# Two-direction state-space stage: one exponential per head, and pairs of heads spread between projections

## The chip, the cores and the metric

One Trainium2 chip, one of its cores. The metric is the device time of one execution in microseconds, shorter being better. A profiled execution gives a trace; its times are the ones quoted below unless a median of runs is named. The engines are called PE (TensorE), DVE (VectorE), ACT (ScalarE), POOL (GpSimd) and SP (SyncE, here the queue that issues nearly all DMAs).

## The reference

Two layers of an encoder over 512 tokens of width 1024. Each layer projects the normalised tokens to everything that three branches need, mixes the branches with sigmoid gates, and ends with an MLP. Only the state-space branch is touched by the change. For every one of 16 heads of width 64, and for each direction, it computes per chunk of 128 tokens

```
a_cum   = cumsum(dt * A)                       # negative, falls along the direction
decay   = exp(where(tril, a_cum[l] - a_cum[s], -inf))
y_diag  = (C B^T * decay) @ (x * dt)           # inside a chunk
states  = B^T @ (x * dt * exp(a_last - a_cum)) # one 64 x 128 state per chunk
s       = s * exp(a_last) + state              # scan over 4 chunks
y_off   = (C @ s_prev) * exp(a_cum)
y       = y_forward + y_backward + x * D,  then * SiLU(z), RMSNorm per group of 8 heads
```

with one dt and one A per head and direction; the backward direction runs on reversed tokens. B and C are shared by the 8 heads of a group, and there are two groups.

## The kernel before

All activations lie features by tokens: a tile is 128 features x 512 tokens. A projection is `feat`: one weight tile of 128x1024 arrives by DMA (`wr`), ACT rounds it to a high part `wh`, another engine computes the low part `wl = wr - wh`, and PE runs 24 matmuls of 512 columns (high x high, high x low, low x high, 8 slices each) into one of two PSUM banks (`pf`). The weights come in a fixed order through three buffers each of `wr`, `wh` and `wl`, so projections run in that order whatever else happens. A scheduler with a model of the engines then fixes each engine's list of instructions; on the chip every engine works through its own list in order and waits on semaphores.

The state-space stage follows the second branch (GLA) in each layer. First come the step sizes `dt` and the cumulated decays `ac` for 32 head-directions (a short chain over DVE, POOL, ACT and PE), written to DRAM as `acd` (the sums) and `ead` (their exponentials). `ssd_group` makes, per group, the transposed B and the product C B^T, masked into two constant tiles: `zt[0]` keeps the upper triangle (forward), `zt[1]` the lower (backward). `ssd_pair` handles two heads: PE transposes x (`xt`), POOL weights it for the states (`xw`), PE forms six chunk states, which ACT copies to `st` and eight DVE instructions scan in place. Then, for each of two heads and two directions, a row of `acd` is broadcast by DMA into a 128x512 tile `E`; DVE subtracts this chunk's column and clamps at 0 (4 instructions of 128x128), ACT exponentiates, DVE multiplies by dt and `zt` (4 instructions); POOL adds the two directions. PE multiplies the result with `xt` into `py`; three matmuls per direction bring in the states, multiplied by a broadcast row of `ead` (`eb`), and POOL adds those onto x.

In the code the four pairs of group 0 come first, then the six convolved projections of group 1 (`ssd_conv`), four pairs, eight gated branch projections (`gate` and `branch`: two projections each), and eight gate projections z (`ssd_gate`). The scheduler moves projections up between pairs. For the weights of group 1's convolutions, of the second branch's gates and projections and of z (the set `on_pool`, 30 tiles a layer) POOL computes `wl`, for all others DVE.

Of the kernel before, what the change touches and what calls it, by code (L numbers as in the profile page):

```python
# [16 lines left out]
P = 128  # L17
NT = 512
# [181 lines left out]
def trunk(tc, a, out, layers=L, dbg=None):  # L200
    nc = tc.nc
    V, S, G, T = nc.vector, nc.scalar, nc.gpsimd, nc.tensor
    with ExitStack() as ctx:
# [75 lines left out]
        on_pool = set()  # L279

        def wprep(l, key):
# [6 lines left out]
            with hp():  # L288
                (G if key in on_pool else V).tensor_tensor(lo, raw, f(hi), ALU.subtract)  # L289
# [94 lines left out]
        for l in range(layers):  # L384
# [23 lines left out]
            on_pool.update(ck_(1) + bk_(1) + [("z", j) for j in range(8)])  # L408
# [367 lines left out]
            def ssd_conv(pxs, g):  # L776
                res = []
                tiles = [("xs", 4 * g + j, 4 * g + j) for j in range(4)] + [("B", g, 8 + g), ("C", g, 10 + g)]
                for n, i, ci in tiles:
                    ps = feat(l, (n, i), xh, xl)  # L780
                    u = evac("cu")
                    with hp():
                        V.tensor_tensor(u, ps, rbc, ALU.mult)
                    o = (px_ if n == "C" else pxs).t("xs" if n == "xs" else "bc")
                    w_ = lambda k: cc(C_CW + 5 * ci + k)
                    S.activation(o, u, AF.Identity, bias=cc(C_CB + ci), scale=w_(2))
                    for k in (0, 1, 3, 4):
                        d = k - 2
                        so = slice(max(0, -d), NT - max(0, d))
                        si = slice(max(0, d), NT - max(0, -d))  # L790
                        V.scalar_tensor_tensor(o[:, so], u[:, si], w_(k), o[:, so], ALU.mult, ALU.add)
                    S.activation(o, o, AF.Silu)
                    res.append(o)
                return res
# [12 lines left out]
            c0 = ssd_conv(px_, 0)  # L807
# [4 lines left out]
            ph = Phase(tc, f"S{l}", {"xt": 2, "bt": 1, "xw": (2, 768), "st": (2, 768), "eb": 4, "to": 1, "E": 6,  # L812
                                     "sm": 2, "z": 2, "xs": 4, "bc": 1},
# [8 lines left out]
            dt, e1, e2, sp, ac, dec, wst = sm[:7]  # L822
            V.tensor_tensor(dt, pdt, cb32(cc(C_DTB, 32)), ALU.add)
# [22 lines left out]
            S.activation(dec, pcs[:, 2], AF.Exp)  # L846
# [26 lines left out]
            def ssd_pair(g, j, t6, bt):  # L873

                x_, Ct, r0 = t6[j], t6[5], 8 * g + 2 * j
# [5 lines left out]

                xw, st = ph.t("xw", (P, 2, 3, P)), ph.t("st", (P, 6, P))
                h2 = lambda ap: ap.rearrange("p c (h e) -> p c h e", h=2)
                for d in range(2):
                    w_ = wst[:, d: d + 3, 16 * d + r0: 16 * d + r0 + 2]
                    G.tensor_tensor(h2(xw[:, d]), h2(xt[:, d: d + 3]), w_.unsqueeze(3).to_broadcast((P, 3, 2, 64)),
                                    ALU.mult)
                for d in range(2):
# [4 lines left out]
                decf = dec.rearrange("p c h -> p (c h)")  # L893
                for n, prev, cur in ((1, (0, 5), (1, 4)), (2, (1, 4), (2, 3))):
                    for d in range(2):
                        c = n if d == 0 else 3 - n
                        for hh in range(2):
                            e = slice(64 * hh, 64 * hh + 64)
                            k = 16 * d + r0 + hh
                            V.scalar_tensor_tensor(st[:, cur[d], e], st[:, prev[d], e], dec[:, c, k: k + 1],  # L900
                                                   st[:, cur[d], e], ALU.mult, ALU.add)
                M = []
                for hh in range(2):
                    md = []
                    for d in range(2):
                        r = 16 * d + r0 + hh
                        e_ = ph.t("E", (P, 4, P))
                        nc.sync.dma_start(flat(e_), acd[r: r + 1, :].to_broadcast((P, NT)))
# [3 lines left out]
                        for c in range(4):  # L912
                            V.scalar_tensor_tensor(e_[:, c], e_[:, c], dt[:, c, r: r + 1], zt[d][:, c],  # L913
                                                   ALU.mult, ALU.mult)
                        md.append(e_)
                    G.tensor_tensor(md[0], md[0], md[1], ALU.add)
                    M.append(md[0])
# [22 lines left out]
            def ssd_gate(g, ys):  # L940
                ss = ph.t("to")
                for j in range(4):
                    ps = feat(l, ("z", 4 * g + j), xh, xl)
                    z_ = ph.t("z")
                    with hp():
                        V.tensor_tensor(z_, ps, rbc, ALU.mult)
# [86 lines left out]
```

## Time and profile before

| | us |
|---|---|
| median of 3 runs (2567.43 to 2570.15) | 2568.5 |
| the profiled execution | 2569.42 |
| its span, first to last instruction | 2567.6 |
| PE busy in the span | 2488.8 |
| DVE busy | 1526.9 |
| ACT busy | 1091.2 |
| POOL busy | 568.3 |

About 1.8 us of the profiled execution lie outside its span. Matmuls are pipelined, so the busy time of PE counts overlapping instructions and waits inside a run of them, and does not say that PE works at its peak: within the state-space stage the count of instructions per microsecond says more. A row of a group gives the busy time and the mean duration; an instruction that is held up after it began counts as busy.

### The profile page before, as it was taken

How to read it: one execution, taken by the hardware profiler on the slowest of the kernel's cores; microseconds unless marked ns; L12 is line 12 of the kernel's file. 1: busy time of each engine (PE TensorE's matmuls, PEld its weight loads, DVE VectorE, ACT ScalarE, POOL GpSimd, SP SyncE). 2: the span in 40 equal slices, each digit the busy share in tenths (PEclk: the TensorE clock that was granted, in tenths of full speed). 3: DMA queues.
4: the chain of work that ended last, by engine and by line, in shares of the span. 5: the costliest groups of instructions: out<-in, count | busy, mean ns of one | idle time of the engine just before them, and what ended most of it. 6: DMA issues, size and time to landing. Idle time of an engine off the chain costs nothing.

```text
span 2567.6 us, 32774 instructions
## 1 busy us (share of the span) xinstructions
PE 2488.8 (97%) x12656; PEld 2086.2 (81%) x12656; DVE 1526.9 (59%) x2468; ACT 1091.2 (43%) x1735; POOL 568.3 (22%) x425
## 2 busy tenths in 40 slices
PE   9999999998879999999999999999978899999999
PEld 7889889877667888888888898898866688888887
DVE  6774534688987553443448745346888875534433
ACT  4565435553335242332436644455533353423322
POOL 3232101236553120000122311011455521100000
PEclk9999999999889999999999999999998899999999
DMA  5222222124332323322332222222243332322332
GB/s 181 92 90 65 84 91 82 67 75 133 112 103 83 123 99 99 99 95 95 126 125 91 91 69 81 83 84 66 74 131 109 99 119 95 101 97 99 99 98 82
DMA packets 84604, 249.39 MB, mean 97 GB/s; under 512 B 9824, under 2 KB 15840, under 8 KB 84448
## 3 DMA queue, kind: packets, MB, share of 16 engines
q1 hardware_dynamic: 84016, 246.85, 29.4%
q8 instruction: 100, 1.64, 0.3%
q14 instruction: 56, 0.46, 0.1%
q10 hardware_dynamic: 432, 0.45, 0.1%
HBM read 242.80 MB, written 4.46 MB: 96 GB/s over the span
## 4 chain that ended last, share of the span: by engine, by line
PE 84%; DVE 11%; issue 2%; POOL 1%; ACT 1%; DMA 1%; SPq 0%; POOLq 0%; ACTq 0%; DVEq 0%
PE pf L306 11%; PE pf L307 11%; PE pf L308 11%; PE F_pf L307 10%; PE F_pf L308 10%; PE F_pf L306 10%; DVE S_E L913 3%; DVE S_E L910 3%; PE pt L324 2%; PE pt L323 2%; PE pt L325 2%; PE N_po L572 2%; DVE S_st L900 1%; PE N_pt L565 1%; DMA S_E<-acd 1%
## 5 line engine op out<-in xcount | busy, mean ns | idle before, releaser
L287 ACT ACTIVATE wh<-wr 128x1024 fp32r<-128x1024 f32 x378 | 400.3, 1059 | 895.2 <-PE F_pf L307 429.7
L289 DVE TENSOR_TENSOR wl<-wr,wh 128x1024 fp32r<-128x1024 f32 x318 | 407.6, 1282 | 181.8 <-ACT wh L287 180.8
L306 PE MATMUL pf<-xh,wh 128*128 128x512 f32 x1232 | 490.6, 399 | 11.8 <-DVE gl L595 5.7
L307 PE MATMUL pf<-xl,wh 128*128 128x512 f32 x1232 | 490.4, 398 | 0.7 <-DVE xl L351 0.7
L308 PE MATMUL pf<-xh,wl 128*128 128x512 f32 x1232 | 488.3, 396 | 0.0
L306 PEld LDWEIGHTS pf<-xh,wh 128*128 128x128 f32 x1232 | 234.6, 191 | 64.2 <-DVE gl L595 6.6
L307 PEld LDWEIGHTS pf<-xl,wh 128*128 128x128 f32 x1232 | 234.6, 190 | 49.5 <-issue 1.8
L308 PEld LDWEIGHTS pf<-xh,wl 128*128 128x128 f32 x1232 | 234.4, 190 | 49.2 <-issue 0.7
L306 PE MATMUL F_pf<-Ah,wh 128*128 128x512 f32 x640 | 248.3, 389 | 0.0
L308 PE MATMUL F_pf<-Ah,wl 128*128 128x512 f32 x640 | 247.7, 389 | 0.0
L307 PE MATMUL F_pf<-Al,wh 128*128 128x512 f32 x640 | 247.7, 389 | 0.0
L308 PE MATMUL F_pf<-xh,wl 128*128 128x512 f32 x512 | 200.0, 391 | 0.0
L307 PE MATMUL F_pf<-xl,wh 128*128 128x512 f32 x512 | 199.2, 389 | 0.0
L306 PE MATMUL F_pf<-xh,wh 128*128 128x512 f32 x512 | 199.2, 389 | 0.0
L289 POOL TENSOR_TENSOR wl<-wr,wh 128x1024 fp32r<-128x1024 f32 x60 | 148.3, 2474 | 115.0 <-ACT wh L287 114.7
L1010 DVE TENSOR_TENSOR F_x<-F_x,F_pf 128x512 f32<-128x512 f32 x64 | 44.0, 687 | 205.6 <-PE F_pf L308 205.6
L324 PE MATMUL pt<-wl,xh 128*128 128x256 f32 x512 | 146.0, 286 | 0.0
L325 PE MATMUL pt<-wh,xl 128*128 128x256 f32 x512 | 145.8, 286 | 0.0
L323 PE MATMUL pt<-wh,xh 128*128 128x256 f32 x512 | 144.8, 284 | 0.0
L306 PEld LDWEIGHTS F_pf<-Ah,wh 128*128 128x128 f32 x640 | 120.1, 188 | 25.1
L308 PEld LDWEIGHTS F_pf<-Ah,wl 128*128 128x128 f32 x640 | 120.1, 188 | 24.9
L307 PEld LDWEIGHTS F_pf<-Al,wh 128*128 128x128 f32 x640 | 120.1, 188 | 24.8
(306 smaller groups left out, 4475.8 us busy)
## 6 DMA issues: line engine op xcount, KB each, us to landing
wr<-pk SPq DMA_DIRECT2D x378, 512.0 KB, 3.3
S_E<-acd SPq DMA_DIRECT2D x64, 256.0 KB, 3.5
N_bias<-bias SPq DMA_DIRECT2D x48, 256.0 KB, 2.9
S_eb<-ead SPq DMA_DIRECT2D x64, 96.0 KB, 2.8
F_x<-xt SPq DMA_DIRECT2D x15, 256.0 KB, 4.8
xd<-F_x SPq DMA_DIRECT2D x8, 256.0 KB, 2.0
F_x<-xd SPq DMA_DIRECT2D x8, 256.0 KB, 5.3
out<-F_x SPq DMA_DIRECT2D x8, 256.0 KB, 2.0
```

What stands on the lines that cost most here:

```text
L287: S.activation(hi, raw, AF.Copy)
L289: (G if key in on_pool else V).tensor_tensor(lo, raw, f(hi), ALU.subtract)
L306: T.matmul(ps, lhsT=hi[:, c], rhs=rh[k], start=k == 0, stop=False)
L307: T.matmul(ps, lhsT=hi[:, c], rhs=rl[k], start=False, stop=False)
L308: T.matmul(ps, lhsT=lo[:, c], rhs=rh[k], start=False, stop=k == KT - 1)
L323: T.matmul(o, lhsT=rh[k][:, s], rhs=hi[:, c], start=k == 0, stop=False)
L324: T.matmul(o, lhsT=rh[k][:, s], rhs=lo[:, c], start=False, stop=False)
L325: T.matmul(o, lhsT=rl[k][:, s], rhs=hi[:, c], start=False, stop=k == KT - 1)
L572: T.matmul(po[r, P * cb: P * (cb + 1)], lhsT=vv[:, v0 + kb, r], rhs=ptS[:, i, kb], start=kb == 0, stop=kb == 1)
L910: V.tensor_scalar(e_[:, c], e_[:, c], ac[:, c, r: r + 1], 0.0, ALU.subtract, ALU.min)
L913: V.scalar_tensor_tensor(e_[:, c], e_[:, c], dt[:, c, r: r + 1], zt[d][:, c], ALU.mult, ALU.mult)
L1010: V.tensor_tensor(xT[j], xT[j], ps, ALU.add)
```

## The change

It recasts the decay of both directions as one. Within a chunk the forward difference is negative below one side of the diagonal and the backward one on the other side, so the smaller of the two is the one that is needed: exp(min(f_i - f_j, b_i - b_j)), times `zt[0]*dt_f + zt[1]*dt_b`. Per head DVE now has 4 instructions for the minimum, ACT applies the remaining column as the bias of its exponential and multiplies both `zt` by the step sizes (12 instructions of 128x128 in all), and DVE adds and multiplies whole 128x512 tiles. The state scan of a pair becomes two multiplications and two additions over both heads and directions. The addition on POOL falls away, and all `wl` are computed on DVE. A pair is cut into `pair_prep`, `pair_states` and `pair_out`, and the code calls projections (`fill`) between them: 6 convolutions, 16 branch projections and 4 of z, from a list. `gate_norm` of group 0 comes before z of group 1.

```
-        on_pool = set()
...
-                (G if key in on_pool else V).tensor_tensor(lo, raw, f(hi), ALU.subtract)
+                V.tensor_tensor(lo, raw, f(hi), ALU.subtract)
...
-            ph = Phase(tc, f"S{l}", {"xt": 2, "bt": 1, "xw": (2, 768), "st": (2, 768), "eb": 4, "to": 1, "E": 6,
-                                     "sm": 2, "z": 2, "xs": 4, "bc": 1},
+            ph = Phase(tc, f"S{l}", {"xt": 2, "bt": 1, "gs": 1, "xw": (2, 768), "st": (2, 768), "eb": 4, "E": 4, "eB": 2,
+                                     "T": 2, "tb": 1, "sm": 2, "xs": 4, "bc": 1, "tm": (1, 256)},
...
+            V.tensor_scalar(nab, ac[:, :, 16:32], -1.0, None, ALU.mult)
+            V.tensor_tensor(wj, ac[:, :, 0:16], ac[:, :, 16:32], ALU.subtract)
...
+                    nc.sync.dma_start(flat(ef), acd[rf: rf + 1, :].to_broadcast((P, NT)))
+                    nc.sync.dma_start(flat(eb_), acd[rb: rb + 1, :].to_broadcast((P, NT)))
+                    t_, tb = ph.t("T", (P, 4, P)), ph.t("tb", (P, 4, P))
+                    for c in range(4):
+                        V.scalar_tensor_tensor(ef[:, c], ef[:, c], wj[:, c, rf: rf + 1], eb_[:, c], ALU.subtract, ALU.min)
+                    for c in range(4):
+                        S.activation(t_[:, c], zt[0][:, c], AF.Copy, scale=dt[:, c, rf: rf + 1])
+                        S.activation(tb[:, c], zt[1][:, c], AF.Copy, scale=dt[:, c, rb: rb + 1])
+                    for c in range(4):
+                        S.activation(ef[:, c], ef[:, c], AF.Exp, bias=nab[:, c, rf: rf + 1])
+                    V.tensor_tensor(t_, t_, tb, ALU.add)
+                    V.tensor_tensor(ef, ef, t_, ALU.mult)
...
-                            V.scalar_tensor_tensor(st[:, cur[d], e], st[:, prev[d], e], dec[:, c, k: k + 1],
-                                                   st[:, cur[d], e], ALU.mult, ALU.add)
...
+                    V.tensor_tensor(he(tm), he(prev), de.unsqueeze(3).to_broadcast((P, 2, 2, 64)), ALU.mult)
+                    V.tensor_tensor(cur, cur, tm, ALU.add)
...
-                            V.tensor_scalar(e_[:, c], e_[:, c], ac[:, c, r: r + 1], 0.0, ALU.subtract, ALU.min)
-                        S.activation(e_, e_, AF.Exp)
-                        for c in range(4):
-                            V.scalar_tensor_tensor(e_[:, c], e_[:, c], dt[:, c, r: r + 1], zt[d][:, c],
-                                                   ALU.mult, ALU.mult)
...
-                    G.tensor_tensor(md[0], md[0], md[1], ALU.add)
...
-            for j in range(4):
-                ssd_pair(0, j, c0, b0)
-            c1 = ssd_conv(ph, 1)
-            b1 = ssd_group(1, c1)
-            for j in range(4):
-                ssd_pair(1, j, c1, b1)
-            for j in range(8):
-                branch(1, j, glh, gll)
-            ssd_gate(0, c0[:4])
-            ssd_gate(1, c1[:4])
...
+            cur = pair_prep(0, 0, c0)
+            fill(2)
+            st = pair_states(0, 0, bts[0], cur[1])
+            for n, (g, j) in enumerate(pairs):
+                nxt = pairs[n + 1] if n < 7 else None
+                if nxt:
+                    if nxt == (1, 0):
+                        bts.append(ssd_group(1, c1))
+                    new = pair_prep(*nxt, cs[nxt[0]])
+                fill(1 + (n > 3))
+                pair_out(g, j, cs[g], cur[0], cur[2], st)
+                fill(1)
+                if nxt:
+                    st = pair_states(*nxt, bts[nxt[0]], new[1])
+                    cur = new
+                fill(1)
+            fill(len(todo))
+            gate_norm(0, c0[:4])
```

The scheduler makes new lists for this code; only those of the state-space stage differ, about as follows in the first layer (the second is alike). On DVE, around the second and third pair, there stood before:

```order
L910 TENSOR_SCALAR S_E_5574<-S_E_5574,S_sm_5154 128x128 [waits DMAHW7_49]
L910 TENSOR_SCALAR S_E_5574<-S_E_5574,S_sm_5154 128x128 x3
L913 SCALAR_TENSOR_TENSOR S_E_5551<-S_E_5551,S_sm_5153,zt_101 128x128 [waits Activation_49]
L913 SCALAR_TENSOR_TENSOR S_E_5551<-S_E_5551,S_sm_5153,zt_101 128x128 [waits DVE_49]
L934 TENSOR_TENSOR S_eb_5410<-S_x_5413,S_eb_5410 128x384 [waits PE_49]
L913 SCALAR_TENSOR_TENSOR S_E_5551<-S_E_5551,S_sm_5153,zt_101 128x128 [waits DVE_49] x2
L913 SCALAR_TENSOR_TENSOR S_E_5562<-S_E_5562,S_sm_5153,zt_103 128x128 [waits Activation_49]
L913 SCALAR_TENSOR_TENSOR S_E_5562<-S_E_5562,S_sm_5153,zt_103 128x128 [waits DVE_49] x3
```

and after the change, for the third pair (minimum, two 128x512 steps per head, the scan of the second pair, and the low part of a weight):

```order
L898 SCALAR_TENSOR_TENSOR S_E_5608<-S_E_5608,S_sm_5157,S_eB_5609 128x128 [waits DMAHW6_49,DMAHW3_49]
L898 SCALAR_TENSOR_TENSOR S_E_5608<-S_E_5608,S_sm_5157,S_eB_5609 128x128 x3
L904 TENSOR_TENSOR S_T_5413<-S_T_5413,S_tb_5414 128x512 [waits Activation_49]
L898 SCALAR_TENSOR_TENSOR S_E_5632<-S_E_5632,S_sm_5157,S_eB_5633 128x128 [waits DMAHW7_49,DMAHW4_49]
L898 SCALAR_TENSOR_TENSOR S_E_5632<-S_E_5632,S_sm_5157,S_eB_5633 128x128 x3
L922 TENSOR_TENSOR S_tm_5552<-S_st_5541,S_sm_5157 128x256 [waits Activation_49]
L905 TENSOR_TENSOR S_E_5409<-S_E_5409,S_T_5413 128x512 [waits DVE_49]
L923 TENSOR_TENSOR S_st_5541<-S_st_5541,S_tm_5552 128x2x128 [waits DVE_49]
L592 TENSOR_TENSOR gl_6176<-pf_6151,rx_213 128x512 [waits PE_49]
L287 TENSOR_TENSOR wl_6199<-wr_6196,wh_6198 128x1024 [waits DMAHW2_49,Activation_49]
```

The four clamps and four products per head and direction have become four minima per head and two long instructions; every row but `gl` takes two inputs from SBUF. On POOL, in the same place, there stood before:

```order
L916 TENSOR_TENSOR S_E_5265<-S_E_5265,S_E_5276 128x512
L289 TENSOR_TENSOR wl_6462<-wr_6459,wh_6461 128x1024
L916 TENSOR_TENSOR S_E_5345<-S_E_5345,S_E_5356 128x512
L886 TENSOR_TENSOR S_xw_5323<-S_xt_5321,S_sm_5154 128x384 x2
L936 TENSOR_TENSOR X_xs_4904<-X_xs_4904,S_eb_5298 128x384
L289 TENSOR_TENSOR wl_6495<-wr_6492,wh_6494 128x1024
L916 TENSOR_TENSOR S_E_5368<-S_E_5368,S_E_5379 128x512
L611 TENSOR_TENSOR mixed_3118<-mixed_3118,gl_6456 128x512
```

and now:

```order
L608 TENSOR_TENSOR mixed_3118<-mixed_3118,gl_6009 128x512
L947 TENSOR_TENSOR X_xs_4904<-X_xs_4904,S_eb_5483 128x384
L947 TENSOR_TENSOR X_xs_4904<-X_xs_4904,S_eb_5492 128x384
L887 TENSOR_TENSOR S_xw_5605<-S_xt_5603,S_sm_5157 128x384 x2
L947 TENSOR_TENSOR X_xs_4944<-X_xs_4944,S_eb_5706 128x384
L947 TENSOR_TENSOR X_xs_4944<-X_xs_4944,S_eb_5715 128x384
```

so that the weighting for the states, the additions onto x and the mixing are left. On SP, the DMA queue, the loads for the third pair stand after the change like this (`S_eB` and `S_E` are the two rows of `acd` for one head, `wr` a weight):

```order
L281 DMA wr_6196<-pk 128x1024 [waits DMAHW2_49,DVE_49]
L895 DMA S_eB_5609<-acd_86 128x512 [waits DMAHW4_49,DMAHW3_49,DVE_49]
L895 DMA S_eB_5633<-acd_86 128x512 [waits DMAHW6_49,DVE_49]
L281 DMA wr_6287<-pk 128x1024 [waits DMAHW5_49,DVE_49]
L894 DMA S_E_5608<-acd_86 128x512 [waits PE_49]
L894 DMA S_E_5632<-acd_86 128x512 [waits DMAHW7_49,PE_49]
```

The load of an `E` now waits until PE has finished `py` of the pair two before (four buffers for four heads), where before it waited mostly for POOL or PE with six buffers for three half-pairs.

Counted in these lists, from the first pair's transposes to the first sum of squares of the gate (`ones` times `ss`), PE runs 456 matmuls of 512 columns before and 436 after, since 20 of them now come ahead of those transposes. Up to the output of the fifth pair (of eight) PE has 209 of the 436, and DVE the minima of 12 heads (48 instructions), 24 long instructions, 20 instructions of the scan and 8 low parts.

## Rows read from the trace of the kernel before

**Rows 1.** The page: the chain that ended last, shares of the span.

```profile
PE 84%; DVE 11%; issue 2%; POOL 1%; ACT 1%; DMA 1%; SPq 0%; POOLq 0%; ACTq 0%; DVEq 0%
```

**Rows 2.** Busy time by stretch: stage in layer 0 (two), dense projections, layer 1.

```profile
core 0: us, PE busy (x) PEld busy (x) DVE busy (x) ACT busy (x) POOL busy (x), PEclk, DMA share, GB/s
600.24:722.87 122.63, 101.22 (x506) 81.31 (x504) 112.13 (x259) 40.44 (x61) 70.76 (x47) 0.87 0.42 130
722.87:791.73 68.86, 60.93 (x311) 49.29 (x312) 57.61 (x119) 23.57 (x36) 41.45 (x30) 0.93 0.26 85
860.00:880.00 20.00, 20.00 (x90) 16.54 (x90) 9.14 (x8) 4.79 (x5) 3.44 (x3) 1.00 0.31 103
1874.13:2068.36 194.23, 161.26 (x818) 129.56 (x817) 170.80 (x376) 64.02 (x97) 112.29 (x77) 0.90 0.38 112
```

**Rows 3.** PE groups, 600.24 to 791.73: busy us, mean ns | idle before, releaser.

```profile
L306 PE MATMUL pf<-xh,wh 128*128 128x512 f32 x96 | 40.6, 423 | 3.0 <-DVE gl L595 3.0
...
L306 PE MATMUL pf<-Ah,wh 128*128 128x512 f32 x56 | 24.2, 432 | 0.9 <-DVE gl L609 0.9
...
L933 PE MATMUL S_x<-X_bc,S_st 128*128 128x128 f32 x96 | 19.3, 325 | 19.5 <-DVE S_st L900 15.7 <-ACT S_st L892 3.7
...
L922 PE MATMUL S_py<-S_E,S_xt 128*64 128x128 f32 x128 | 13.0, 312 | 4.9 <-POOL S_E L916 3.2 <-issue 1.6
```

**Rows 4.** Timeline of PE: start, us, line, operation, count.

```profile
606.40 1.50 PE L891 MATMUL S_x<-S_xw,S_bt 128*128 128x128 f32 x12
...
662.06 1.09 PE L922 MATMUL S_py<-S_E,S_xt 128*64 128x128 f32 x16
```

**Rows 5.** DVE groups, 600.24 to 791.73.

```profile
L913 DVE SCALAR_TENSOR_TENSOR S_E<-S_E,S_sm,zt 128x128 f32<-128x128 f32 x128 | 57.3, 511 | 0.2 <-ACT S_E L911 0.2
L910 DVE TENSOR_SCALAR S_E<-S_E,S_sm 128x128 f32<-128x128 f32 x128 | 52.3, 468 | 6.5 <-DMA S_E<-acd 6.5
L900 DVE SCALAR_TENSOR_TENSOR S_st<-S_st,S_sm 128x64 f32<-128x64 f32 x64 | 27.6, 483 | 3.0 <-ACT S_st L892 3.0
```

**Rows 6.** Timeline of DVE.

```profile
613.29 0.86 DVE L900 SCALAR_TENSOR_TENSOR S_st<-S_st,S_sm 128x64 f32<-128x64 f32 x4
...
642.88 3.23 DVE L913 SCALAR_TENSOR_TENSOR S_E<-S_E,S_sm,zt 128x128 f32<-128x128 f32 x12
646.03 4.10 DVE L900 SCALAR_TENSOR_TENSOR S_st<-S_st,S_sm 128x64 f32<-128x64 f32 x4
...
650.85 0.47 DVE L910 TENSOR_SCALAR S_E<-S_E,S_sm 128x128 f32<-128x128 f32 x2
```

**Rows 7.** Timeline of POOL; in brackets the idle time before.

```profile
614.38 2.40 POOL L289 TENSOR_TENSOR wl<-wr,wh 128x1024 fp32r<-128x1024 f32 x1 [7.85 <-ACT wh L287]
...
645.20 2.11 POOL L916 TENSOR_TENSOR S_E<-S_E,S_E 128x512 f32<-128x512 f32 x1 [4.09 <-ACT S_st L892]
647.27 2.39 POOL L289 TENSOR_TENSOR wl<-wr,wh 128x1024 fp32r<-128x1024 f32 x1
```

**Rows 8.** POOL groups, 600.24 to 791.73.

```profile
L289 POOL TENSOR_TENSOR wl<-wr,wh 128x1024 fp32r<-128x1024 f32 x19 | 45.9, 2417 | 25.4 <-ACT wh L287 25.3
L916 POOL TENSOR_TENSOR S_E<-S_E,S_E 128x512 f32<-128x512 f32 x16 | 24.0, 1501 | 32.6 <-ACT S_E L911 10.7 <-ACT S_st L892 7.9 <-DVE S_E L913 6.5
```

**Rows 9.** ACT group, 600.24 to 791.73.

```profile
L911 ACT ACTIVATE S_E<-S_E 128x512 f32<-128x512 f32 x32 | 20.1, 630 | 78.9 <-DVE S_E L910 67.4 <-POOL wl L289 8.7 <-issue 2.8
```

**Rows 10.** ACT groups of the whole span; L635 scales by a column, L848 does not.

```profile
L635 ACT ACTIVATE G_gvg<-pt,tcol 128x256 f32<-128x256 f32 x64 | 26.8, 470 | 29.2 <-PE pt L325 29.1
...
L848 ACT ACTIVATE S_sm<-S_sm 128x128 f32<-128x128 f32 x2 | 0.6, 298 | 0.0
```

**Rows 11.** DVE groups of the whole span.

```profile
L289 DVE TENSOR_TENSOR wl<-wr,wh 128x1024 fp32r<-128x1024 f32 x318 | 407.6, 1282 | 181.8 <-ACT wh L287 180.8
...
L348 DVE TENSOR_TENSOR Al<-F_v,Ah 128x512 fp32r<-128x512 f32 x64 | 43.9, 692 | 0.0
```

**Rows 12.** The page: DMA issues, KB each, median us to landing.

```profile
S_E<-acd SPq DMA_DIRECT2D x64, 256.0 KB, 3.5
```

More of the change, by code (lines that the diff above doesn't have):

```diff
@@ L407, in trunk @@
             order.extend((l, k) for k in ks)
-            on_pool.update(ck_(1) + bk_(1) + [("z", j) for j in range(8)])
             if l == 0:
@@ L774, in gla_out, with conv_tile @@
                     gll.append(l_)
[L776 to L794, printed above, removed]
+            def conv_tile(pxs, n, i, ci):
+                ps = feat(l, (n, i), xh, xl)
+                u = evac("cu")
+                with hp():
+                    V.tensor_tensor(u, ps, rbc, ALU.mult)
+                o = (px_ if n == "C" else pxs).t("xs" if n == "xs" else "bc")
+                w_ = lambda k: cc(C_CW + 5 * ci + k)
+                S.activation(o, u, AF.Identity, bias=cc(C_CB + ci), scale=w_(2))
+                for k in (0, 1, 3, 4):
+                    d = k - 2
+                    so = slice(max(0, -d), NT - max(0, d))
+                    si = slice(max(0, d), NT - max(0, -d))
+                    V.scalar_tensor_tensor(o[:, so], u[:, si], w_(k), o[:, so], ALU.mult, ALU.add)
+                S.activation(o, o, AF.Silu)
+                return o
+            conv_list = lambda g: [("xs", 4 * g + j, 4 * g + j) for j in range(4)] + [("B", g, 8 + g), ("C", g, 10 + g)]
             cur = gla_proj(0)
@@ L845, in trunk @@
                 V.tensor_copy(ac[:, :, r], pcs[:, d, :, r])
-            S.activation(dec, pcs[:, 2], AF.Exp)
+            V.tensor_scalar(nab, ac[:, :, 16:32], -1.0, None, ALU.mult)
+            V.tensor_tensor(wj, ac[:, :, 0:16], ac[:, :, 16:32], ALU.subtract)
+            S.activation(dec[:, 0:2, 0:16], pcs[:, 2, 1:3, 0:16], AF.Exp)
+            for n in range(2):
+                S.activation(dec[:, n, 16:32], pcs[:, 2, 2 - n, 16:32], AF.Exp)
             V.tensor_tensor(wst, pcs[:, 2], ac, ALU.subtract)
@@ L871, in ssd_group, with pair_prep @@
                 return bt
[L873 to L875 removed]
+            def pair_prep(g, j, t6):
+                x_, r0 = t6[j], 8 * g + 2 * j
                 ps = ph.p("x", (P, 4, P))
@@ L887, in ssd_pair, with pair_states @@
                                     ALU.mult)
+                M = []
+                for hh in range(2):
+                    rf, rb = r0 + hh, 16 + r0 + hh
+                    ef, eb_ = ph.t("E", (P, 4, P)), ph.t("eB", (P, 4, P))
+                    nc.sync.dma_start(flat(ef), acd[rf: rf + 1, :].to_broadcast((P, NT)))
[10 more added lines that the diff above has]
+                    V.tensor_tensor(ef, ef, t_, ALU.mult)
+                    M.append(ef)
+                return xt, xw, M
+            def pair_states(g, j, bt, xw):
+                r0 = 8 * g + 2 * j
+                st = ph.t("st", (P, 6, P))
                 for d in range(2):
@@ L963, in ssd_gate, with fill @@
                     sdl.append(l_)
-            b0 = ssd_group(0, c0)
-            for j in range(4):
-                ssd_pair(0, j, c0, b0)
-            c1 = ssd_conv(ph, 1)
-            b1 = ssd_group(1, c1)
-            for j in range(4):
-                ssd_pair(1, j, c1, b1)
-            for j in range(8):
-                branch(1, j, glh, gll)
-            ssd_gate(0, c0[:4])
-            ssd_gate(1, c1[:4])
+            c1, todo = [], []
+            for k in conv_list(1):
+                todo.append(lambda k=k: c1.append(conv_tile(ph, *k)))
+            for j in range(8):
+                todo.append(lambda j=j: gls.append(gate(1, j)))
+                todo.append(lambda j=j: branch(1, j, glh, gll, gls.pop(0)))
+            for j in range(4):
+                todo.append(lambda j=j: gate_tile(0, j, c0[:4]))
+            gls = []
+            def fill(n=1):
+                for _ in range(min(n, len(todo))):
+                    todo.pop(0)()
+            pairs = [(g, j) for g in range(2) for j in range(4)]
+            bts, cs = [ssd_group(0, c0)], [c0, c1]
+            cur = pair_prep(0, 0, c0)
[16 more added lines that the diff above has]
+            gate_norm(0, c0[:4])
+            for j in range(4):
+                gate_tile(1, j, c1[:4])
+            gate_norm(1, c1[:4])
             ph.close()
```

59 lines of the change are left out of this document (26 added, 33 removed).

## The prediction

> **What bounds the kernel now.** I read the page's chain first: 84% of what ended last is PE, and 11% is DVE [rows 1]. So PE sets the pace nearly everywhere, and the question is where DVE does. The chain in order of time puts the DVE pieces between about 600 and 790 us, and again about 1275 us later in the second layer: the state-space stage. Next I compared stretches [rows 2]. In dense projections PE runs 90 matmuls of 512 columns in 20 us, 0.222 us each, at the full granted clock. From the first pair's transposes (600.24) to the first sum of squares of the gate (791.73) there are 122.63 + 68.86 = 191.5 us, in which DVE is busy for 112.13 + 57.61 = 169.7 us and PE's granted clock averages 0.87 and then 0.93. The second layer's stretch is 194.2 us with the same picture.
>
> What would PE need there? The two L306 forms are a third each of their projections, so there are 3 x (96 + 56) = 456 long matmuls, 101.2 us at 0.222. Of the 817 instructions 96 are L933, 96 L891 (12 per pair), 128 L922 and 41 others [rows 2 to 4]. At 1.50/12 = 0.125 us and 1.09/16 = 0.068 us, both with the tail of their group in them, they take 233 x 0.125 + 128 x 0.068 = 37.8 us. PE's floor is 139 us. The stage loses 52 us in the first layer and 55 in the second, 107 in all: no change of this stage alone can bring more. Part of it are waits (L933 waits 15.7 us for the state scan [rows 3]), the rest is the clock at its lower level (1.2 instead of 2.4 GHz) after such waits, and small steps.
>
> **Why DVE is so slow there.** The same four scan instructions take 0.86 us at 613.29, where POOL has been idle for 7.85 us until 614.38, and 4.10 us from 646.03, while POOL works from 645.20 to 649.66 [rows 6, 7]. Twelve products take 3.23 us just before, with POOL idle for 4.09 us until 645.20. So these instructions stand still while POOL works. Alone they would cost 128 x 0.27 (L913) + 128 x 0.235 (L910, 0.47/2) + 64 x 0.215 (L900) = 78.4 us; they were busy for 57.3 + 52.3 + 27.6 = 137.2 us [rows 5, 6]. The difference of 59 us is 52% of POOL's 112.2 us in the stretch [rows 2].
>
> The Trainium skill states this as a rule (SBUF — State Buffer, sections SBUF: two separate sides and Terms: VectorE instructions that use two ports or take two SBUF inputs and GpSimd share one port pair, which is locked for a whole instruction, the loser blocking fully). The 4.10 us row agrees. The rule speaks against counting too much: the new minima, sums and scan steps have two SBUF inputs as well, so they stay exposed. By the rule at its worst all POOL time in the first five pairs lands on DVE, not half; that is 12 us a layer more, and 2540 instead of the forecast below.
>
> **What is removed, added and moved (per layer, in this stretch).** DVE loses 137.2 us and keeps 169.7 - 137.2 = 32.5 us. It gains 64 minima, 32 long instructions (add and product), 32 scan steps and 19 low parts. Prices: a minimum is a two-tensor instruction with a column over 128, like L913 alone: 0.27. A long one is L348: 0.69, a low part 1.28 [rows 11]. A scan step over 256 columns is not in the trace; it lies between 0.27 (128 columns) and 0.69 (512), and I take 0.41, a third of the way. That is 17.3 + 22.1 + 13.1 + 24.3 = 76.8, so 109 us without holding. POOL loses 45.9 + 24.0 us [rows 8] and keeps 112.2 - 69.9 = 42.3; 52% of it is 22 us. DVE: about 131 us against 170, under PE's floor of 139 on average. The stage would then be PE's, if the work were spread evenly.
>
> It is not. The lists put five pairs (with preparation of a sixth) beside 209 long matmuls, and three pairs beside 227. For the first part, DVE: 48 x 0.27 + 24 x 0.69 + 20 x 0.41 + 8 x 1.28 = 48.0; five eighths of the 32.5 kept, 20.3; holding 0.52 x 5/8 x 42.3 = 13.7; waits for `E`, where I keep the 6.5 us that L910 shows [rows 5]; and a lag at the start, when the transposes are done and the first rows of `acd` are still on their way: one landing of 3.5 us [rows 12] and four issues, 4.5 us. Sum: 93 us. PE's floor in the same part: 209 x 0.222 + 5/8 x 37.8 = 70. DVE sets the pace, by 23 us. Second part, PE: 227 x 0.222 + 3/8 x 37.8 = 64.6; DVE is some 50 us there, so I add only 4 us for chains that are late once in a while.
>
> The 20 matmuls that come ahead of the transposes cost 20 x 0.222 = 4.4 us before 600.24 is reached. So the stretch ends after 4.4 + 93 + 64.6 + 4 = 166 us instead of 191.5: 25.5 us less. The second layer starts from 194.2: 28 us less. Together 53.5 us.
>
> Costed at nothing: ACT. It loses 32 exponentials (20.1 us) that waited 78.9 us, mostly for DVE [rows 9], and gains 24 small instructions a pair. One over 128 columns with a column operand is not in the trace; L848 (128, no column) takes 0.298, L635 (256, with a column) 0.470 [rows 10]. Between them, 0.37, it is 8.9 us a pair; the 64.0 - 20.1 = 43.9 us that ACT keeps add 5.5, 14.4 in all, against 93/5 = 18.6 for DVE. It is hidden while DVE is the slower of the two; the cover is 4 us a pair, and at 0.470 only 1.8. The SP queue carries two loads of `acd` per head as before. The four `E` buffers instead of six make a load wait for `py` two pairs back; behind the waiting load stand `ead` loads and a weight, and DVE's list has between 3 and 6 instructions (2 to 3 us) between that pair's output and the first minimum that needs the load, against 3.5 us to landing. That is the 6.5 us kept. The step-size chain ahead of the stage loses POOL's low parts that stood between its steps; DVE gets them, and PE had other projections to run: nothing either way. The low parts later in the stage ask 1.28 us of DVE in each 5.3 us projection (24 x 0.222).
>
> **The rivals.**
> *PE's floor (chance 0.22).* Neighbouring DVE instructions overlap, holding falls more than POOL's time does, and only some 8 us a layer stay above 139: 191.5 - 147 and 194.2 - 147, 92 us less, 2478; I put this case at 2475 to 2498. For it: the mean rows are prices with their tails. Against it: the uneven lists.
> *ACT takes over (0.17).* Twelve instructions a head in 12 heads at 0.470 are 68 us, with 5 x 5.5 = 27 of its other work 95 us; and since ACT's products wait for one buffer `tb` that DVE must free, DVE's holding (13.7) adds to it instead of hiding: 109 us for the first part, 182 for the stretch, 9 and 12 us gained: 2548. The Trainium skill (ScalarE: Activation LUTs, Rules for kernel authors) says to put plain multiplications on VectorE rather than ScalarE; here DVE is the engine that is waited for, and ACT waits 78.9 us for it, which speaks for the move as far as the cover above goes. No run here shows the small instructions themselves.
> *Slower: the reloads (0.08).* `eB` has two buffers, `E` four, and SP issues in order. If each of the 12 heads of the first part waits a whole landing of 3.5 us, that is 42 us instead of 6.5: the stretch is 201.5 us, and the kernel is 17 us slower, about 2586. It turns slower when the waits exceed 6.5 + 25.5 = 32 us, 2.7 us a head. Against it: most loads of `eB` are issued a pair ahead in the list.
> *No change (0.03).* The removed DVE time comes back entirely as low parts and waits, within 0.2% (5 us, about what runs of this kernel can tell).
>
> **How the numbers follow.** The likeliest case (0.50) gives 2569.4 - 53.5 = 2516 for the profiled execution, which was 0.9 us above the median of the runs shown, so 2515 for a median. Its own range, with the scan step between 0.27 and 0.69 (-3 and +6 us a layer in the first part), the waits for `E` between 0 and twice 6.5, and holding at 40 to 70%, is about 2495 to 2537. Eight times in ten: from inside the floor case, 2480, to just past the ACT case, 2553. Faster by over 0.2%: 0.50 + 0.22 + 0.17 less a little for the weak end of the ACT case, 0.87; within 0.2% 0.05; slower 0.08.
>
> **What would show it.** Right: DVE's busy time in the stretch falls from 170 to some 130 us, POOL's from 112 to 42; the first five pairs take about 93 us, the other three with their projections about 69; the state-scan wait of L933 shrinks below 5 us; the granted clock rises above 0.95 in the second part and stays below 1 in the first. A minimum shows 0.27 alone and more under POOL. Wrong: DVE instructions with two SBUF inputs held for more than half of POOL's time; small ACT instructions near 0.47 us with DVE idle for ACT; DVE idle for `S_E<-acd` or `S_eB<-acd` by more than 30 us a layer; projections waiting for `wl`; or a change outside the stage, which the lists exclude.

## The result, and the profile after

| | us |
|---|---|
| before, median of 4 runs (2567.11 to 2570.15) | 2567.97 |
| after, median of 4 runs (2467.42 to 2469.90) | 2468.97 |
| ratio, 95% interval | 0.9613 (0.9596 to 0.9629) |
| profiled execution before, after | 2569.42, 2469.90 |

The kernel became 99 us faster; the forecast was 53.5, and 2469 lies below the range (2480 to 2553). The direction was right, the size too small by 46 us. The chain that ended last answers to [rows 1]: DVE's 11% have gone to 1%.

```profile
PE 96%; DMA 2%; DVE 1%; ACT 1%; issue 0%; SPq 0%; DVEq 0%
```

Busy time by stretch, answering to [rows 2]: from the first pair's transposes (601.09) to the output of the fifth pair (681.13), and from there to the first sum of squares of the gate (745.26), and below them the whole way from the transposes to the second sum of squares (769.51), by which kernels are compared from here on, since the same work lies ahead of its end in all of them.

```profile
core 0: us, PE busy (x) PEld busy (x) DVE busy (x) ACT busy (x) POOL busy (x), PEclk, DMA share, GB/s
601.09:681.13 80.04, 76.67 (x448) 62.55 (x447) 71.30 (x130) 67.18 (x183) 29.95 (x24) 0.98 0.59 181
681.13:745.26 64.13, 64.13 (x356) 53.61 (x355) 47.76 (x73) 34.28 (x75) 22.06 (x18) 1.00 0.33 105
...
601.09:769.51 168.42, 165.05 (x907) 135.87 (x906) 137.41 (x224) 117.77 (x277) 57.73 (x45) 0.99 0.44 138
```

To the first sum of squares it is 80.04 + 64.13 = 144.2 us where [rows 2] has 191.5. That point came 791.73 - 745.26 = 46.5 us earlier in the first layer, and 2068.36 - 1968.95 = 99.4 earlier in the second: 53 us more. From the second sum of squares of one layer to the transposes of the next it is 1057.1 us before and 1057.9 after (20 matmuls have moved ahead of the transposes), so all of the gain lies in the two stages, as the lists said it would. (A correction to [rows 2]: the first pair's transposes of the kernel before begin at 599.57 us, and 600.24 is the second long matmul behind them. The table further down starts at 599.57.)

The PE groups that answer to [rows 3], from 601.09 to 745.26. L944 is the old L933 (the states into the output), L933 the old L922 (`py`). The 15.7 us in which the output waited for the scan are gone.

```profile
L944 PE MATMUL S_x<-X_bc,S_st 128*128 128x128 f32 x96 | 14.4, 287 | 0.0
...
L933 PE MATMUL S_py<-S_E,S_xt 128*64 128x128 f32 x128 | 12.0, 297 | 1.3 <-DVE S_E L905 1.3
```

What PE waited for in the whole first-layer stage:

```profile
PE pf L304 <- DVE gl L592: 2.1, 1, 2.1
PE S_py L933 <- DVE S_E L905: 1.3, 1, 1.3
```

DVE in the first five pairs (601.09 to 681.13), answering to [rows 5]: busy us, mean ns, idle before and its releaser.

```profile
L898 DVE SCALAR_TENSOR_TENSOR S_E<-S_E,S_sm,S_eB 128x128 f32<-128x128 f32 x48 | 15.9, 392 | 7.6 <-DMA S_eB<-acd 5.0 <-DMA S_E<-acd 1.4 <-issue 1.0
L905 DVE TENSOR_TENSOR S_E<-S_E,S_T 128x512 f32<-128x512 f32 x12 | 10.6, 881 | 0.1
L904 DVE TENSOR_TENSOR S_T<-S_T,S_tb 128x512 f32<-128x512 f32 x12 | 10.0, 836 | 0.0
L287 DVE TENSOR_TENSOR wl<-wr,wh 128x1024 fp32r<-128x1024 f32 x8 | 9.9, 1238 | 0.0
L923 DVE TENSOR_TENSOR S_st<-S_st,S_tm 128x256 f32<-128x256 f32 x10 | 5.9, 594 | 0.1
L922 DVE TENSOR_TENSOR S_tm<-S_st,S_sm 128x256 f32<-128x256 f32 x10 | 4.6, 464 | 0.7 <-ACT S_st L917 0.7
```

The reader is to see three things. DVE is busy for 71.3 of 80.0 us, so it no longer fills this part. Its idle time (7.6 us at the minima) is mostly the first pair's loads. And the mean prices are above the ones that stand alone in the timeline of the same stretch, where POOL was idle until 616.91, and from 618.53 to 626.93. DVE, then POOL:

```profile
611.45 0.69 DVE L904 TENSOR_TENSOR S_T<-S_T,S_tb 128x512 f32<-128x512 f32 x1
613.93 1.14 DVE L898 SCALAR_TENSOR_TENSOR S_E<-S_E,S_sm,S_eB 128x128 f32<-128x128 f32 x4 [1.79 <-DMA S_eB<-acd]
...
621.05 0.41 DVE L922 TENSOR_TENSOR S_tm<-S_st,S_sm 128x256 f32<-128x256 f32 x1
...
616.91 1.62 POOL L887 TENSOR_TENSOR S_xw<-S_xt,S_sm 128x384 f32<-128x384 f32 x2 [8.39 <-ACT S_xt L882]
626.93 1.27 POOL L608 TENSOR_TENSOR mixed<-mixed,gl 128x512 f32<-128x512 f32 x1 [8.39 <-DVE gl L606]
```

### The profile page after: what moved, and what is told of

It is laid out like the page before. It is cut to its first block, busy times and chain, and to the rows that moved or that the text cites. A ratio compares the mean times of both kernels' runs of the same rounds, so it can differ in the third digit from the quotient of the medians.

```text
span 2468.1 us, 32626 instructions
## 1 busy us (share of the span) xinstructions
PE 2452.2 (99%) x12656; PEld 2064.9 (84%) x12656; DVE 1425.8 (58%) x2148; ACT 1162.1 (47%) x2055; POOL 393.3 (16%) x333
## 4 chain that ended last, share of the span: by engine, by line
PE 96%; DMA 2%; DVE 1%; ACT 1%; issue 0%; SPq 0%; DVEq 0%
PE pf L304 14%; PE pf L305 14%; PE pf L306 14%; PE F_pf L306 11%; PE F_pf L305 11%; PE F_pf L304 11%; PE pt L322 3%; PE pt L321 2%; PE pt L323 2%; PE N_po L569 2%; PE N_pt L562 1%; PE S_x L944 1%; PE G_at L699 1%; PE S_py L933 1%; PE G_at L700 1%; PE S_x L916 1%
## 5 line engine op out<-in xcount | busy, mean ns | idle before, releaser
L287 DVE TENSOR_TENSOR wl<-wr,wh 128x1024 fp32r<-128x1024 f32 x378 | 485.7, 1285 | 188.4 <-ACT wh L285 186.6
L1044 DVE SCALAR_TENSOR_TENSOR F_v<-F_pf,rx 128x512 f32<-128x512 f32 x64 | 44.1, 691 | 159.5 <-PE F_pf L306 159.5
```

The lines of the kernel that those rows point to most:

```text
L287: V.tensor_tensor(lo, raw, f(hi), ALU.subtract)
L1044: V.scalar_tensor_tensor(v_, ps, 0.0, rbc, ALU.max, ALU.mult)
```

## The experiments

### The change taken apart: arithmetic, low parts, order

The change has three parts that can be taken one by one: the arithmetic of a pair (minimum, step sizes on ACT, the scan), the low parts `wl` of 30 weights per layer on DVE instead of POOL, and the order (pairs in steps with projections between them). The first four runs do each part alone, and all but the low parts. Three theories stood against each other: A, DVE's time is what counts, and the low parts are even; B, POOL's holding of DVE is the loss; C, the order is what counts.

`wl_back`, the changed kernel with

```
-                V.tensor_tensor(lo, raw, f(hi), ALU.subtract)
+                (G if key in on_pool else V).tensor_tensor(lo, raw, f(hi), ALU.subtract)
```

> The changed kernel, with the low parts of the 30 weights per layer back on POOL. If DVE's time in the stage is what counts (theory A), DVE loses 18 x 1.14 = 20.5 us of its own work in the stretch and pays 0.31 to 0.52 of POOL's 45.9 us more in holding, 14 to 24 us: about even, and PE is near its floor anyway; the time is 2463 to 2482. If the gain comes from POOL's silence (theory B: the 59 us of holding are what the old stage lost), some 30 us a layer come back: about 2530.

Measured 2498.59, ratio 0.9725 (0.9710 to 0.9739): 30 us of the 99 come back. Neither theory's number: about half of B's.

`wl_alone`, the kernel before with the opposite edit:

> The kernel before, with all low parts on DVE and nothing else changed. Theory A: DVE gets 19 x 1.28 = 24 us of work more in the stretch and is relieved of 0.52 x 45.9 = 24 us of holding: no change, 2560 to 2580. Theory B: holding was the loss, 24 to 40 us a layer are gained: 2490 to 2520.

Measured 2520.41, 0.9811 (0.9797 to 0.9826): this one line alone gives 49 us. Theory A fails here.

`arith_alone`, the kernel before with the new body of the pair and the new scan, in the old order (z in the `eB` buffers, as in the changed kernel):

```
-                            V.tensor_scalar(e_[:, c], e_[:, c], ac[:, c, r: r + 1], 0.0, ALU.subtract, ALU.min)
-                        S.activation(e_, e_, AF.Exp)
...
+                        V.scalar_tensor_tensor(ef[:, c], ef[:, c], wj[:, c, rf: rf + 1], eb_[:, c], ALU.subtract, ALU.min)
...
-                    z_ = ph.t("z")
+                    z_ = ph.t("eB")
```

> The kernel before, its code order and its low parts on POOL, but with the new decay, step sizes on ScalarE and the new state scan. Theory A: DVE's time in the stretch falls from 170 to about 110 to 120 us, below PE's 139, so most of the gain is here: 2485 to 2510. Theory C (the order of the work between projections is what counts; a pair's chain of transposes, states, scan and output has nothing beside it in the old order): less than a third of the 99 us, 2535 to 2568.

Measured 2502.84, 0.9740 (0.9723 to 0.9756): the largest part, 66 us.

`order_alone`, the changed kernel with the same lines the other way round (`E` 6), the old scan, and the low parts on POOL as in `wl_back`:

> The changed kernel's order (pairs in three steps with projections between them), with the old decay, the old scan and POOL's low parts. Theory A: DVE still needs some 170 us in a stretch in which PE needs 139, so no more than 20 us a layer can be gained: 2530 to 2568. Theory C: most of the 99 us, 2480 to 2505, with PE's granted clock above 0.97 in the stretch.

Measured 2561.32, 0.9972 (0.9961 to 0.9984): 8 us; DVE is busy for 190.8 of the stage's 212.6 us there. Theory C alone fails.

The parts give 66 + 49 + 8 = 123 us apart and 99 together, so they overlap. Two of them at a time, `order_wl` (the old body and scan in the new order, low parts on DVE) and `arith_wl` (the new ones in the old order, low parts on DVE):

> The changed kernel's order and all low parts on DVE, with the old decay and the old scan. Theory D (formed on the first four runs: POOL's low parts cost by holding DVE, and by the steps of a pair that stand behind them; the order is worth only what it was worth alone, some 8 us): 2520 less 0 to 15, 2505 to 2520. Theory C2 (the order pays once DVE is no longer held): 2480 to 2500.

Measured 2515.98, 0.9790 (0.9774 to 0.9806), as theory D said: with the old arithmetic DVE is still too slow, and the order adds 4 us.

> The old order, with the new decay and scan and all low parts on DVE: the change without its order. Theory D: DVE's time is 137.6 + 22 - 0.74 x 48 = 124 us in a stretch that ends with the second sum of squares and takes PE 165, so nearly all is gained without the order: 2468 to 2480. Theory C2: the waits of the old order stay (scan, 7.3 us a layer, and the clock behind them): 2485 to 2500.

Measured 2497.48, 0.9719 (0.9705 to 0.9733): theory D fails. The eight kernels in one table (median us):

| arithmetic | order | low parts on POOL | low parts on DVE |
|---|---|---|---|
| old | old | 2568 | 2520 |
| old | new | 2561 | 2516 |
| new | old | 2503 | 2497 |
| new | new | 2499 | 2469 |

With the old arithmetic the low parts are worth 45 to 48 us and the order 4 to 8. With the new, each alone is worth 4 to 5 us, and both together 34. An interval reaches some 4 us to either side, so differences of 2 to 5 us between two of these kernels are at the edge of what the runs tell; the 34 are not. To see why, the stage of each, from its first transposes to its second sum of squares: before, then with the low parts moved (`wl_alone`), then the new arithmetic in the old order (`arith_alone`). The columns are those of the table of stretches above.

```profile
599.57:816.63 217.06, 187.34 (x928) 150.87 (x927) 189.50 (x399) 80.91 (x119) 118.39 (x81) 0.91 0.35 110
```

```profile
600.37:792.38 192.01, 172.92 (x910) 137.43 (x909) 175.73 (x409) 85.45 (x120) 80.07 (x61) 0.98 0.38 122
```

```profile
602.06:789.82 187.76, 175.65 (x941) 144.08 (x940) 137.59 (x209) 121.71 (x281) 97.44 (x64) 0.97 0.41 128
```

In the second, DVE has taken 17 low parts more (28.6 us in its rows against 5.6), and is still busy for 13.8 us less: the rest of its work fell by 36.8 us, for 38.3 us that POOL works less. In the third, DVE is down to 137.6 us, below PE's need; what is left are waits of PE, 11.9 us in all and at most 5.1 at a time, and the lower clock behind some of them (a mean of 0.97). What PE waited for there is named in the traces of the two kernels that lack one part. In `wl_back` (new order, low parts on POOL) it is DVE's late decay, and once a late evacuation of the output:

```profile
PE S_py L936 <- DVE S_E L908: 6.4, 2, 4.5
PE S_x L883 <- DVE S_eb L948: 2.5, 1, 2.5
```

In `arith_wl` (old order, low parts on DVE) a z projection waits for an evacuation that stands in DVE's list behind minima whose `E` was not loaded: the load was issued at 715.75, after `py` had freed one of the four buffers (714.05) and behind a weight and two rows of `ead` in SP's list. So I took that away (`"E": 6`):

> The run arith_wl (new arithmetic, all low parts on DVE, old order) with six E buffers instead of four. In its trace PE and DVE stand still once per layer behind loads of E that wait for py (about 715 to 724 us, DVE 4.5 us, and PE at the lower clock behind it). Theory F (the old order loses by the buffers only): the 12 to 14 us a layer that it lacks come back, 2470 to 2478. Theory C (the old order itself leaves PE without work for a pair's chain): 2487 to 2498.

Measured 2494.96, 0.9711 (0.9696 to 0.9725): in theory C's range; the buffers were worth 2 us or nothing. The wait for the z evacuation is still there, together with waits for POOL's weighting, and the clock behind it at 0.69 of full speed from 710 to 720 us:

```profile
PE pf L306 <- DVE S_eB L949: 4.1, 1, 4.1
PE S_x L895 <- POOL S_xw L890: 2.1, 2, 1.8
PE pf L306 <- DVE gl L594: 1.6, 3, 0.6
...
710.00:720.00 10.00, 5.77 (x17) 0.69 0.26 92
```

This does not show yet that it is the order. In the runs with the new arithmetic in the old order, z has no buffers of its own: it takes the two of `eB`, and in the old code order these come free only with the minima of the last pair. DVE of `arith_wl_E6` shows it, the last eight minima and the first evacuation of z behind them:

```profile
711.27 1.14 DVE L912 SCALAR_TENSOR_TENSOR S_E<-S_E,S_sm,S_eB 128x128 f32<-128x128 f32 x4 [0.88 <-DMA S_E<-acd]
...
713.27 1.13 DVE L912 SCALAR_TENSOR_TENSOR S_E<-S_E,S_sm,S_eB 128x128 f32<-128x128 f32 x4
714.32 0.68 DVE L949 TENSOR_TENSOR S_eB<-pf,rx 128x512 f32<-128x512 f32 x1
```

In `wl_alone`, where z has its own two buffers in the same order, three evacuations of z (728.15, 737.00, 743.46) run ahead of the last products with `zt` (until 755.8). No run gave z its own buffers beside the new arithmetic, so the order and the shared buffers are not separated.

### What it is in POOL's work that costs

In these two runs DVE keeps the low parts, and POOL, after each of them, works on the used weight buffer; its result is not used. `on_pool` holds the same 30 weights per layer as before. This is `dummy_tt`; `dummy_set` has `G.memset(raw, 0.0)` in the last line.

```
                 V.tensor_tensor(lo, raw, f(hi), ALU.subtract)
+            if key in on_pool:
+                with hp():
+                    G.tensor_tensor(raw, raw, raw, ALU.subtract)
```

> The changed kernel, in which POOL, once DVE has made the low part of one of the same 30 weights, subtracts the used weight buffer from itself (128x1024, two inputs from SBUF), as long as its low part took; its result is not used. Theory D: DVE is held as in the run with POOL's low parts and has those besides: 2495 to 2520. Theory E (the low part came late from POOL, and projections waited for it): the low parts are DVE's here, so the time stays at 2469 to 2476.

> As the run before, but POOL fills the used weight buffer with zeros (writes only). If holding needs POOL to read SBUF, DVE's minima stay at 0.27 us beside it, and only POOL's queue is longer: 2469 to 2480. If any work of POOL holds DVE, or if it is the queue that counts (xw and the additions onto x behind 2.4 us), the time is that of the run before.

Measured 2505.29, 0.9749 (0.9734 to 0.9763), and 2473.32, 0.9625 (0.9611 to 0.9639). No projection waits for POOL in either, so theory E (late low parts) is not needed; reading costs 36 us, writing 4 or nothing. The two are not quite alike in length (2.07 us and 0.95), and in the first layer the subtractions delay the transposes by 14.4 us, of which 42 x 0.226 = 9.5 are matmuls that moved ahead. The other 4.9 us, of the 16.1 by which this layer's second sum of squares came later, are lost before the stage, where the step-size chain's small steps on POOL stand between the subtractions (587.84 to 605.71, in the changed kernel 580.43 to 589.46), so not all of the 36 us is holding. But the timeline shows holding directly. In `dummy_tt`, four minima began at 644.13 and took 3.81 us. Taken one by one, the first three ended at 644.76, 646.66 and 647.68, each 0.15 us after an instruction of POOL (644.61, 646.51 and 647.53; the middle one is a subtraction); the fourth took 0.34. An instruction with a PSUM input just before them (643.67) took its usual 0.54 us beside POOL. POOL and DVE of `dummy_tt`:

```profile
642.69 1.92 POOL L953 TENSOR_TENSOR X_xs<-X_xs,S_eb 128x384 f32<-128x384 f32 x1
644.57 1.94 POOL L292 TENSOR_TENSOR wr<-wr 128x1024 f32<-128x1024 f32 x1
646.48 1.05 POOL L953 TENSOR_TENSOR X_xs<-X_xs,S_eb 128x384 f32<-128x384 f32 x1
...
643.67 0.54 DVE L951 TENSOR_TENSOR S_eb<-S_x,S_eb 128x384 f32<-128x384 f32 x1
644.13 3.81 DVE L904 SCALAR_TENSOR_TENSOR S_E<-S_E,S_sm,S_eB 128x128 f32<-128x128 f32 x4
```

With the fill, two instructions with two SBUF inputs ran at their usual 0.41 and 0.68 us while POOL wrote. POOL and DVE of `dummy_set`:

```profile
658.20 0.96 POOL L292 MEMSET wr<- 128x1024 f32 x1 [1.34 <-DVE wl L289]
...
658.06 0.41 DVE L928 TENSOR_TENSOR S_tm<-S_st,S_sm 128x256 f32<-128x256 f32 x1
658.39 0.68 DVE L911 TENSOR_TENSOR S_E<-S_E,S_T 128x512 f32<-128x512 f32 x1
```

### ACT's part, the buffers, the scan

Three runs of the changed kernel with one edit each. `dve_scale`, the step sizes applied on DVE:

```
-                        S.activation(t_[:, c], zt[0][:, c], AF.Copy, scale=dt[:, c, rf: rf + 1])
-                        S.activation(tb[:, c], zt[1][:, c], AF.Copy, scale=dt[:, c, rb: rb + 1])
+                        V.tensor_scalar(t_[:, c], zt[0][:, c], dt[:, c, rf: rf + 1], None, ALU.mult)
+                        V.tensor_scalar(tb[:, c], zt[1][:, c], dt[:, c, rb: rb + 1], None, ALU.mult)
```

> The changed kernel, with the 8 multiplications of zt by the step sizes per head done on DVE (128x128, one tile and a column) instead of ScalarE. DVE gets 12 x 8 x 0.235 = 22.6 us in the first five pairs, where it is busy 71 of 80 us: 94 us with its waits of today, 12 to 20 us a layer more: 2493 to 2510. If ScalarE sets the pace of the heads (the rival that it takes over), no slower than 2469 to 2475.

Measured 2492.83, 0.9705 (0.9690 to 0.9720): 24 us of the gain hang on ACT doing this. DVE is then busy for 77.6 of the 80 us from 601 to 681, and PE waits 7.3 us behind that, between 715 and 727:

```profile
601.00:681.00 80.00, 77.00 (x427) 62.38 (x426) 77.62 (x178) 38.16 (x81) 24.64 (x19) 1.00 0.56 171
```

`eB1` (`"eB": 1` instead of 2):

> The changed kernel with one eB buffer instead of two: each load of a backward row waits until the head before has its minima. If a landing of 3.5 us per head shows (the rival of the reloads), the 12 heads of the first part lose up to 42 us a layer: 2500 to 2550. If DVE has other work for the time of a landing, as the trace of the changed kernel shows after its first pair (0.2 to 1.3 us of waiting a pair), some 5 us a layer: 2470 to 2485.

Measured 2485.97, 0.9677 (0.9661 to 0.9693): 17 us, between the two. DVE's minima wait 21.9 us for rows of `acd` in a layer, where they wait 8.0 in the changed kernel (64 minima, to the first sum of squares):

```profile
L898 DVE SCALAR_TENSOR_TENSOR S_E<-S_E,S_sm,S_eB 128x128 f32<-128x128 f32 x64 | 22.3, 402 | 21.9 <-DMA S_eB<-acd 12.9 <-DMA S_E<-acd 8.9
```

`old_scan` (the old eight steps of 128x64 per pair, all else as changed):

> The changed kernel with the old state scan: eight steps of 128x64 per pair for four instructions of 128x256. Alone they cost the same (8 x 0.215 = 1.72 us against 4 x 0.42 = 1.68 us a pair): 2467 to 2475. If the scan's place in the pair's chain is what the old kernel lost by (15.7 us of waits of its output matmuls), 2480 to 2500.

Measured 2474.43, 0.9633 (0.9619 to 0.9648): the new scan is worth some 5 us at the edge of the intervals, inside the first range; the old one's 64 steps are busy for 22.0 us against 8.9 + 8.5 for the new ones.

## Why the prediction was wrong

**What held.** DVE's busy time was the lever, and it fell below PE's need. To the first sum of squares DVE is busy for 71.3 + 47.8 = 119.1 us (forecast 131, before 169.7). A minimum shows 0.27 us in a run of four (1.14 together). The output's wait for the scan is gone, the clock is 1.00 in the second part and 0.98 in the first. A scan step alone takes 0.41, the value I chose. One of ACT's new instructions takes 0.39 us (0.37 assumed), in all three of its groups. Outside the two stages the time is the same within 1 us.

**The step that failed: "DVE sets the pace, by 23 us".** I gave the first five pairs 93 us on DVE, and they took 80.0, term by term:

| first five pairs, us | forecast | measured |
|---|---|---|
| new work, as it stands alone | 48.0 | 47.4 |
| held by POOL | 13.7 | 9.5 |
| work kept, by its rows | 26.6 | 20.5 |
| overlap of neighbours | -6.3 | -6.1 |
| waits for loads and the lag | 11.0 | 8.7 |
| sum | 93.0 | 80.0 |

Four terms were too large: the kept work by 5.9 us (26.6 - 6.3 = 20.3 against 20.5 - 6.1 = 14.4), the holding by 4.2, the waits by 2.3 and the prices by 0.6. New work alone is 48 x 0.27 + 24 x 0.68 + 20 x 0.42 + 8 x 1.22, with a minimum at its step within a run and the others at their middle durations in the trace; the six groups above add up to 56.9, and the difference to 47.4 is the holding, 9.5 us or 32% of POOL's 29.95. The groups of DVE in this part add up to 77.4, while DVE is busy for 71.3: an instruction begins some 0.08 us before the one ahead of it ends (621.05 + 0.41 is past 621.38, where the next one stands).

The 20.3 of kept work in the forecast came from 169.7 - 137.2, busy time less rows of groups. The rows of all groups of that stretch add up to 179.8, so the old kernel's overlap of 10.0 us had been taken off with it: by rows, 42.6 us were kept, five eighths of which are 26.6, with 6.3 of overlap. The overlap of another set of instructions came out nearly the same; that was luck. The kept work did not, because five eighths of everything was the wrong share. Of the 42.6 us, 12.4 are the evacuations of z and the products with it, which all stand behind the fifth pair (before, 600.24 to 791.73):

```profile
L948 DVE TENSOR_TENSOR X_xs<-X_xs,S_z 128x512 f32<-128x512 f32 x4 | 6.6, 1660 | 2.8 <-ACT S_z L947 2.8
L946 DVE TENSOR_TENSOR S_z<-pf,rx 128x512 f32<-128x512 f32 x5 | 3.4, 686 | 5.6 <-PE pf L308 5.6
L948 DVE TENSOR_TENSOR S_xs<-S_xs,S_z 128x512 f32<-128x512 f32 x1 | 2.4, 2398 | 0.7 <-ACT S_z L947 0.7
```

PE then waited only 3.4 us; its own 76.7 us (forecast 70) set the pace. Of the difference, 0.26 x 5 + 0.08 x 5 = 1.7 us are the lower clock behind the two waits (0.74 and 0.92 of full speed in the two stretches of 5 us from 621 to 631); the rest I did not take apart.

**The other pieces of the first layer's 21 us.** The second part took 64.1 us against 68.6: the 4 us for late chains were not needed. The transposes began at 601.09, 1.5 us later than before and not 4.4: two waits of PE of 1.5 us each ahead of them (for the step-size chain and for ACT) are gone, where I had said nothing either way. Counted from 600.24, as the forecast does, that is 3.5 us: 2.9, and the 0.7 by which that start was too late. 13.0 + 4.5 + 3.5 = 21.0, and 25.5 + 21.0 is the 46.5 us measured. The second layer gave 53 us for 28; its PE waited 2.2 us, and I did not split it into pieces.

**The holding share.** I took 52%, a mean over the old stage, as a price. It is no constant. Taking POOL's low parts from the old kernel freed 36.8 us on DVE for 38.3 on POOL, 96%; putting them back into the changed one cost 26.6 us for 42.2, 63% (DVE is busy for 140.2 us, with 5.2 instead of 29.0 of them low parts); the added subtractions cost 15.1 for 35.6, 42%. Whether a POOL instruction meets a DVE instruction that it can hold depends on what DVE has queued. With 52% I priced the low parts as even, and they were worth 49 us alone; the time that they gave back in the old kernel is 24 us a layer, for 13.8 us of DVE's busy time. PE's wait for the scan went from 15.7 to 2.2 us too, and the clock rose with it: by the mean granted clock of the two rows above, (1 - 0.91) x 217.06 less (1 - 0.98) x 192.01, some 16 us of the 24 are an estimate of what the lower clock cost. My price had only DVE's time in it. How much of the shorter waits came from DVE's holding and how much from POOL's shorter queue (the weighting of x and the additions stood behind low parts) was not separated in the old kernel.

For a VectorE instruction with two SBUF inputs, the Trainium skill (SBUF — State Buffer, SBUF: two separate sides) limits the holding to a GpSimd instruction that reads SBUF; the two dummy runs agree, 3.81 us for four minima beside POOL's reading instructions and the usual 0.68 for a product beside a fill. The 2540 that I made of that rule at its worst, with all of POOL's time on DVE, was wrong: the share was 32% in the first five pairs of the changed kernel.

**The rivals.** PE's floor (chance 0.22, 2475 to 2498) is what happened, and further than I put it: counted from 600.24, the first sum of squares came after 145.0 us against 147, and in the second layer 53 us were gained against 47. Of its two reasons, holding did fall by more than POOL's time; the overlap did not grow (8.3 us to the first sum of squares, 10.0 before). ACT did not take over: it is busy for 67.2 of the first 80 us, and taking its work away costs 24 us. The advice of the Trainium skill (ScalarE: Activation LUTs, Rules for kernel authors), plain multiplications on VectorE, would have been wrong here by that amount, since DVE was the one with little room. The reloads are covered with two `eB` buffers; with one they cost 17 us, so the rival's mechanism exists and its place was wrong. "No change" and "slower" did not come near.

**What stays open.** Why order and low parts are worth 34 us together and 4 to 5 apart is shown only as far as the waits and the clock go. In the first layer, `wl_back` reaches the second sum of squares 12.7 us after the changed kernel (782.20 against 769.51) and `arith_wl` 15.6 us after it (785.10). PE stands still for 9.8 and 12.4 us in their stages against 3.4. The granted clock averages 0.97 over 181.56 and 0.96 over 184.93 us against 0.99 over 168.42, by which I estimate 4 and 6 us more at the lower clock. Together that is some 10 of the 12.7 us and 15 of the 15.6. The waits are in other places in each kernel, no run took them away one by one, and in `arith_wl` the longest may belong to the buffers that z shares and not to the order.

## What to carry to other kernels

Where two engines hold each other up, price an instruction by what it takes when the other is idle, and price the holding by the instructions that will actually meet; a share averaged over the old kernel was off by a factor of 1.6 to 1.8, in both directions. When an engine's new total comes near the bound engine's, count for each part of a stage what the lists put there, the work that stays included: an even share of it was the largest error here. Do not mix rows of groups with busy time, which differ by the overlap of neighbours (179.8 against 169.7 us). And parts of a change that seem worth nothing alone can be the ones that let the last waits disappear, so take them out of the finished kernel as well as adding them to the old one.

## What the runs showed of the hardware

POOL instructions that only write SBUF did not hold DVE: 17.2 us of fills in the stage left DVE's busy time at 136.5 us (137.4 without them). DVE holds POOL as well: in the changed kernel one `mixed` (L608) began at 647.64 and took 3.14 us where most take 1.27 to 1.30, while DVE ran three instructions with two SBUF inputs one behind the other (647.48 to 649.63). DVE instructions with one input from PSUM and one from SBUF were not held: L945 has a mean of 546 ns after, 547 before and 543 with the subtractions, and none of the 32 in any of these runs took over 0.56 us. An instruction with one tile and a column from SBUF was held too: the multiplications of `dve_scale` (L900, L901) took 0.27 us where no POOL instruction ran beside them, and 0.70 and 0.86 in the mean where one did. Whether the column or something else in them is the reason, these runs cannot tell.
